# A page table fetched in one transfer and sorted on the chip, in place of 20 small transfers

## The chip, the cores and the metric

The kernel runs on one core of a Trainium2 chip. The metric is the device time of one execution in microseconds (us). Before the change its median over three runs is 2779.84 us (2775.24 to 2781.72).

## The reference: what is computed

One inference step of a two-layer hybrid decoder: a prompt of 16 + 512 tokens and a sample group of 8 sequences with 8 new tokens each, 592 tokens in all, with a model width of 1024. Each layer is a feed-forward block, a mixer and a second feed-forward block. The mixer joins a state-space scan with an attention of eight heads. The sample group's attention also reads 2048 older keys and values for each sequence from a paged cache:

```python
page_table (8, 16) int32          # page_table[b, g]: physical page of sequence b's g-th block of 128 tokens
k_past = cache_k[l][page_table].reshape(8, 2048, 8, 64)
v_past = cache_v[l][page_table].reshape(8, 2048, 8, 64)
```

The page table has 128 entries and is the same for both layers. It is first used in the mixer of layer 0; the feed-forward block that comes ahead of it doesn't need it.

## The kernel before, in words

Activations lie with the model dimension on the 128 partitions and the 592 tokens along the free dimension, as eight tiles `x`. Precision is kept by splitting: each operand becomes a rounded high part and the remainder (`xh`, `xl` for activations, `whi`, `wlo` for weights), and each product is three matmuls, `whi` by `xh`, `whi` by `xl`, `wlo` by `xh` (`mm3`, L585 to L593, two halves of 296 columns).

Weights come in as `raw` tiles of 512 KB (`raw`, L570; three buffers), all issued from SyncE's queue (SP). Each serves two sets of 24 matmuls. For each set ScalarE (ACT) writes `whi` (L581), VectorE (DVE) subtracts and writes `wlo` (L582), and TensorE (PE) multiplies; `whi` and `wlo` have three buffers each. Two PSUM banks hold a pair of halves, and three pairs are in turn.

The norm's factor R, one number a token, is worked out beside the first matmuls: `sq` holds summed squares (L453), matmuls sum them over partitions (L463), ACT copies the sums (L471), PE transposes them (L476), DVE works out a reciprocal root in small steps (`rs`, `rv`, `ry`, `rw`, L494 to L515), PE spreads it (L206), ACT writes `R` (L559). Until R is there no product may leave PSUM (L229 multiplies by R), so PE can fill three pairs and then stands.

`setup` loads the activations; `setup_rest` (L275) prepares all that only the mixer needs and is called from within the first feed-forward block, after the first of its three parts. Each engine works through its own list in order and waits on semaphores. A scheduler that simulates the program fixes the order of each list when the program is built; so an instruction whose inputs seem to be there early can stand in the list long ahead of the place where the source has it.

Two page-table tiles feed the index tiles of the gathers, `ki` (keys, L347) and `vi` (values, L351). Partition p of `ptk` holds, for each of the 8 sequences, the entry of block p // 8; partition p of `ptv` holds, for each sequence and each of four values of a, the entry 4a + p // 32. Both are filled straight from HBM: 16 transfers of 8 partitions by 8 elements (L332) and 4 transfers of 32 partitions by 32 elements (L335), in which neighbours along a partition are not neighbours in HBM. DVE then converts them to float (`kf` L338, `vf` L339), and scales and offsets them (L340 to L351). GpSimd (POOL) issues the gathers (L1462, L1526) in the mixer.

`dtr` (L984) is a small weight tile of the scan, with its split `dtw` on ACT (L989) and DVE (L990); `mt` (L286) holds masks and `dk` (L294) a skip factor.

Of the kernel before, what the change touches and what calls it, by code (L numbers as in the profile page):

```python
# [11 lines left out]
I32 = mybir.dt.int32  # L12
AF = mybir.ActivationFunctionType
ALU = mybir.AluOpType
# [13 lines left out]
def const_arrays():  # L28
    p = np.arange(128)
    f = np.float32  # L30
    a32 = np.arange(32)
    c = {}
    c["ident"] = np.eye(128)
    c["ones"] = np.ones((128, 1))
    c["half"] = p[:, None] // 64 == np.arange(32)[None, :]
    o8 = np.zeros((128, 64))
    q64 = np.arange(64)
    same = q64[:, None] // 8 == q64[None, :] // 8
    o8[:64] = same
    c["one8"] = o8  # L40
    c["srep"] = p[:, None] % 32 == p[None, :] % 32
    a16 = np.arange(16)[None, :]
    c["sel16"] = (p[:, None] % 8 == a16 % 8) & (p[:, None] // 32 % 2 == a16 // 8)
    c["mko"] = ((p[:, None] // 8) % 4 == np.arange(4)[None, :])
    sm = np.zeros((128, 8))
    sm[:64] = q64[:, None] // 8 == np.arange(8)[None, :]
    c["seqm"] = sm
    dsel = np.zeros((128, 8))
    for h in range(8):
        dsel[h, h] = 1.0  # L50
        dsel[32 + h, h] = 1.0
    c["dsel"] = dsel
    c["koff"] = ((p % 8) * 16)[:, None]
    c["voff"] = ((p % 32) * 4)[:, None]
    c["kt16"] = np.broadcast_to(np.arange(16)[None, :], (128, 16))
    return {k: np.ascontiguousarray(v.reshape(128, -1)).astype(f) for k, v in c.items()}

# [47 lines left out]
class Kern:  # L105
# [169 lines left out]
    def setup_rest(self):  # L275
        nc, I = self.nc, self.I
# [4 lines left out]
        n = off["tri"][0]  # L281
# [43 lines left out]
            nc.vector.tensor_copy(o[:, 0], v)  # L325
            nc.vector.tensor_scalar(o[:, 1], v, -1.0, None, ALU.mult)

        ptk = self.cst([128, 8], "ptk", I32)
        ptv = self.cst([128, 32], "ptv", I32)
        pt = I["page_table"]  # L330
        for g in range(16):
            nc.sync.dma_start(ptk[8 * g:8 * g + 8, :], pt[:, g].partition_broadcast(8))  # L332
        ptr = pt.rearrange("b (a x) -> x (b a)", x=4)
        for x in range(4):
            nc.sync.dma_start(ptv[32 * x:32 * x + 32, :], ptr[x].partition_broadcast(32))  # L335
        kf = self.cst([128, 8], "kf")
        vf = self.cst([128, 32], "vf")
        nc.vector.tensor_copy(kf, ptk)  # L338
        nc.vector.tensor_copy(vf, ptv)  # L339
        nc.vector.tensor_scalar(kf, kf, 128.0, self.c_koff, ALU.mult, ALU.add)  # L340
        nc.vector.tensor_scalar(vf, vf, 128.0, self.c_voff, ALU.mult, ALU.add)
        nc.vector.tensor_scalar(kf, kf, 0.5, None, ALU.mult)
# [1230 lines left out]
def build(nc, inputs):  # L1573
    arrays, I, O = {}, {}, {}
    CA, CM = pack(const_arrays()), pack(mask_arrays())
    given = {k: np.ascontiguousarray(inputs[k]) for k in _INS}
    given["c_const"], given["c_mask"] = CA[1], CM[1]
    for name, a in given.items():
        arrays["in_" + name] = a
        I[name] = nc.dram_tensor("in_" + name, a.shape, mybir.dt.from_np(a.dtype), kind="ExternalInput").ap()  # L1580
    for name, shape in _OUTS:
        O[name] = nc.dram_tensor("out_" + name, shape, F32, kind="ExternalOutput").ap()
    with tile.TileContext(nc, schedule_with_timeline_sim=True) as tc:
        with ExitStack() as ctx:
            Kern(tc, ctx, I, O, CA, CM).run()
    return arrays
# [10 lines left out]
```

## Time and profile before

| | |
|---|---|
| median of three runs | 2779.84 us |
| the profiled execution | 2797.72 us |
| its span, first to last instruction | 2795.9 us (1.8 us lie around it) |
| mean granted TensorE clock | 0.973 |
| PE busy | 2656.9 us (95% of the span) |
| DVE busy | 1502.2 us (54%) |
| ACT busy | 994.7 us (36%) |
| POOL busy | 356.9 us (13%) |
| transfers from SP's queue | 213184 packets, 205.71 MB |

A row of the timeline gives start, duration, engine, line and operation, output and inputs; in square brackets stands how long the engine had been idle and what ended that. "PEclk" is the granted TensorE clock as a share of full speed, and "x" in a table of windows counts instructions. The rows that matter stand in the prediction.

### The profile page before, as it was taken

How to read it: one execution, taken by the hardware profiler on the slowest of the kernel's cores; microseconds unless marked ns; L12 is line 12 of the kernel's file. 1: busy time of each engine (PE TensorE's matmuls, PEld its weight loads, DVE VectorE, ACT ScalarE, POOL GpSimd, SP SyncE). 2: the span in 40 equal slices, each digit the busy share in tenths (PEclk: the TensorE clock that was granted, in tenths of full speed). 3: DMA queues.
4: the chain of work that ended last, by engine and by line, in shares of the span. 5: the costliest groups of instructions: out<-in, count | busy, mean ns of one | idle time of the engine just before them, and what ended most of it. 6: DMA issues, size and time to landing. Idle time of an engine off the chain costs nothing.

```text
span 2795.9 us, 51271 instructions
## 1 busy us (share of the span) xinstructions
PE 2656.9 (95%) x21469; PEld 2472.6 (88%) x21469; DVE 1502.2 (54%) x2978; ACT 994.7 (36%) x1795; POOL 356.9 (13%) x336
## 2 busy tenths in 40 slices
PE   6999999999877999999999999999997789999999
PEld 5999999887655899999999999998885568999999
DVE  4444445386768564343554343454776776444444
ACT  2222224255645332222332222233565543322222
POOL 1000000023356010000000000000334541000000
PEclk8999999999979999999999999999998899999999
DMA  3232234347677222222222322244576772222222
GB/s 100 76 93 93 79 106 134 113 145 258 204 233 241 100 69 85 82 76 88 72 84 76 105 77 92 87 145 126 169 248 203 250 236 69 78 89 80 88 77 87
DMA packets 250279, 343.22 MB, mean 123 GB/s; under 512 B 38104, under 2 KB 201888, under 8 KB 250048
## 3 DMA queue, kind: packets, MB, share of 16 engines
q1 hardware_dynamic: 213184, 205.71, 23.8%
q0 software_dynamic: 36864, 134.23, 14.4%
q8 instruction: 168, 2.75, 0.4%
q14 instruction: 63, 0.52, 0.1%
HBM read 320.23 MB, written 19.66 MB: 122 GB/s over the span
## 4 chain that ended last, share of the span: by engine, by line
PE 59%; DVE 3%; ACT 2%; DMA 1%; issue 1%; POOL 0%; another core or an unknown queue 0%; SPq 0%; DVEq 0%; ACTq 0%; POOLq 0%
PE g L590 52%; PE v L905 1%; DMA v<-in_cache_v,vi 1%; DVE kt L1468 1%; PE po L206 1%; PE po L463 0%; PE po L209 0%; PE sc L209 0%; DMA kn<-in_cache_k,ki 0%; PE z L209 0%; POOL v L1526 0%; PE z L206 0%; ACT L1090 0%; ACT dec L1090 0%; DVE x L777 0%
## 5 line engine op out<-in xcount | busy, mean ns | idle before, releaser
L590 PE MATMUL g<-xh,wlo 128*128 128x296 f32 (+1 forms) x3392 | 1014.6, 300 | 17.3 <-DVE wlo L582 17.3
L590 PE MATMUL g<-xl,whi 128*128 128x296 f32 (+1 forms) x3392 | 1015.9, 300 | 2.7 <-DVE xl L441 2.7
L590 PE MATMUL g<-xh,whi 128*128 128x296 f32 (+1 forms) x3392 | 1014.7, 300 | 2.4 <-DVE gs L229 2.0
L581 ACT ACTIVATE whi<-raw 128x512 fp32r<-128x512 f32 (+1 forms) x664 | 413.9, 624 | 1342.5 <-PE g L590 1271.1
L582 DVE TENSOR_TENSOR wlo<-raw,whi 128x512 fp32r<-128x512 f32 (+1 forms) x664 | 450.9, 679 | 614.5 <-ACT whi L581 568.4
L590 PEld LDWEIGHTS g<-xh,wlo 128*128 128x128 f32 x3392 | 640.4, 189 | 20.6 <-DVE wlo L582 17.9
L590 PEld LDWEIGHTS g<-xh,whi 128*128 128x128 f32 x3392 | 640.0, 189 | 10.5 <-issue 6.3
L590 PEld LDWEIGHTS g<-xl,whi 128*128 128x128 f32 x3392 | 640.5, 189 | 7.5 <-DVE xl L441 3.6
L590 PE MATMUL g<-hl,whi 128*128 128x296 f32 (+1 forms) x1408 | 417.9, 297 | 0.0
L590 PE MATMUL g<-hh,wlo 128*128 128x296 f32 (+1 forms) x1408 | 417.7, 298 | 0.0
L590 PE MATMUL g<-hh,whi 128*128 128x296 f32 (+1 forms) x1408 | 416.8, 298 | 0.0
L1462 POOL DMA_INDIRECT kn<-in_cache_k,ki x128 | 134.7, 1052 | 1590.6 <-PE g L590 1104.8
L590 PEld LDWEIGHTS g<-hl,whi 128*128 128x128 f32 x1408 | 265.2, 188 | 0.0
L590 PEld LDWEIGHTS g<-hh,wlo 128*128 128x128 f32 x1408 | 264.3, 188 | 0.0
L590 PEld LDWEIGHTS g<-hh,whi 128*128 128x128 f32 x1408 | 263.9, 188 | 0.0
L1468 DVE STREAM_TRANSPOSE kt<-kn 128x512 f32<-128x512 f32 x256 | 162.9, 681 | 29.0 <-PE pS L1097 7.5
L1526 POOL DMA_INDIRECT v<-in_cache_v,vi x128 | 139.1, 1087 | 252.3 <-DVE kt L1468 121.3
L686 DVE SCALAR_TENSOR_TENSOR x<-g,x 128x296 f32<-128x296 f32 (+1 forms) x192 | 88.2, 464 | 120.5 <-PE g L590 119.9
L229 DVE TENSOR_TENSOR us<-g,R 128x296 f32<-128x296 f32 (+1 forms) x176 | 81.5, 464 | 128.0 <-PE g L590 127.9
L229 DVE TENSOR_TENSOR gs<-g,R 128x296 f32<-128x296 f32 (+1 forms) x176 | 80.7, 464 | 125.9 <-PE g L590 120.0
L673 ACT ACTIVATE hh<-us 128x592 fp32r<-128x592 f32 (+1 forms) x88 | 61.4, 698 | 63.3 <-DVE us L671 63.3
L209 PE MATMUL sc<-kt,qbd 128*32 128x128 f32 x1920 | 79.0, 291 | 3.7 <-issue 3.6
(387 smaller groups left out, 2993.2 us busy)
## 6 DMA issues: line engine op xcount, KB each, us to landing
raw<-in_ffn_w_gu SPq DMA_DIRECT2D x176, 512.0 KB
raw<-in_ffn_w_down SPq DMA_DIRECT2D x80, 512.0 KB
raw<-in_w_in SPq DMA_DIRECT2D x44, 512.0 KB
raw<-in_w_out SPq DMA_DIRECT2D x16, 512.0 KB
spill<-x SPq DMA_DIRECT2D x16, 296.0 KB
x<-spill SPq DMA_DIRECT2D x16, 296.0 KB
raw<-in_ffn_w_down SPq DMA_DIRECT2D x16, 256.0 KB
xt<-in_x_prompt SPq DMA_DIRECT2D x8, 256.0 KB
```

Source lines behind the costliest of these rows:

```text
L206: i = self.nc.tensor.matmul(*a, **k).ins
L209: i = self.nc.tensor.matmul(*a, **k).ins
L229: self.nc.vector.tensor_tensor(tv[0:P, h, :], ps[h][0:P, 0:self.n], rv[0:P, h, :], ALU.mult)
L581: nc.scalar.activation(hi[:, 0:nk], s, AF.Copy)
L582: nc.vector.tensor_tensor(lo[:, 0:nk], s, hi[:, 0:nk].bitcast(F32), ALU.subtract)
L590: nc.tensor.matmul(ps[h][:, 0:self.n], w[:, k, :], self.hv(x)[:, h, :], start=(first and k == 0 and i == 0), stop=(last and k == nk - 1 an ...
L673: nc.scalar.activation(hh[:, a:b], u[:, a:b], AF.Copy)
L686: nc.vector.scalar_tensor_tensor(v, p, 0.5, v, ALU.mult, ALU.add)
L905: nc.tensor.matmul(ps[c], x[:, t0:t0 + 128], w.rearrange("p x c -> p (x c)"), start=(k == 0 and i == 0), stop=(k == 7 and i == 2))
L1462: nc.gpsimd.indirect_dma_start(kn, None, self.kflat, bass.IndirectOffsetOnAxis(ap=self.kidx[l][:, s, i:i + 1], axis=0))
L1468: nc.vector.transpose(kt[:, 2 * u:2 * u + 2].rearrange("p t h i -> p t (h i)"), kns[u][:, :, 256 * quad:256 * quad + 256])
L1526: nc.gpsimd.indirect_dma_start(v.rearrange("p k c -> p (k c)"), None, self.vflat, bass.IndirectOffsetOnAxis(ap=self.vidx[l][:, i, e:e + 1] ...
```

## The change

One transfer brings the whole page table, 128 numbers of 4 bytes, to every one of the 128 partitions (`pti`). DVE converts it to float (`ptf`) and picks what each partition needs: it multiplies by a 0/1 mask (`mg` for keys, `mx` for values, two new constants of 16 and 4 columns) and adds halves together until one entry is left for each output, five instructions for `kf` and three for `vf`. The tiles `ptk` and `ptv` with their 20 transfers go. `pti`, `ptf` and `sel` come from a pool of six rotating buffers that other temporaries use too. What follows (scaling, `ki`, `vi`, the gathers) stays. After the change the lines from L55 to L327 stand 2 further down, and those from L340 on 6 further down.

```diff
+    c["mg"] = p[:, None] // 8 == a16
+    c["mx"] = p[:, None] // 32 == np.arange(4)[None, :]
...
-        ptk = self.cst([128, 8], "ptk", I32)
-        ptv = self.cst([128, 32], "ptv", I32)
-        pt = I["page_table"]
-        for g in range(16):
-            nc.sync.dma_start(ptk[8 * g:8 * g + 8, :], pt[:, g].partition_broadcast(8))
-        ptr = pt.rearrange("b (a x) -> x (b a)", x=4)
-        for x in range(4):
-            nc.sync.dma_start(ptv[32 * x:32 * x + 32, :], ptr[x].partition_broadcast(32))
+        pti = self.tmp("pti", [128, 128], I32)
+        nc.sync.dma_start(pti, I["page_table"].rearrange("b g -> (b g)").partition_broadcast(128))
+        ptf, sel = self.tmp("ptf", [128, 128]), self.tmp("sel", [128, 128])
+        nc.vector.tensor_copy(ptf, pti)
         kf = self.cst([128, 8], "kf")
         vf = self.cst([128, 32], "vf")
-        nc.vector.tensor_copy(kf, ptk)
-        nc.vector.tensor_copy(vf, ptv)
+        for out, m in ((kf, self.c_mg), (vf, self.c_mx)):
+            n, k = out.shape[1], m.shape[1]
+            sv = sel.rearrange("p (a g) -> p a g", g=k)
+            nc.vector.tensor_tensor(sv, ptf.rearrange("p (a g) -> p a g", g=k),
+                                    m.unsqueeze(1).to_broadcast([128, n, k]), ALU.mult)
+            while k > 1:
+                k //= 2
+                d = out.unsqueeze(2) if k == 1 else sv[:, :, 0:k]
+                nc.vector.tensor_tensor(d, sv[:, :, 0:k], sv[:, :, k:2 * k], ALU.add)
```

The engines' lists, built anew, differ in two places. The first is the start. SP's list before, with all 20 page-table transfers (`raw` are weights of the first feed-forward block, `hp` small head parameters):

```order
L278 DMA call<-in_c_const 128x278
L305 DMA hp<-in_dt_bias 128x16
L305 DMA hp<-in_A_log 128x16
L305 DMA hp<-in_sb_bias 128x16
L332 DMA ptk<-in_page_table 8x8x1 x9
L572 DMA raw<-in_ffn_w_gu 128x4x256
L332 DMA ptk<-in_page_table 8x8x1 x7
L572 DMA raw<-in_ffn_w_gu 128x4x256
L335 DMA ptv<-in_page_table 32x32x1 x4
L984 DMA dtr<-in_w_in 128x8x8
L572 DMA raw<-in_ffn_w_gu 128x4x256
```

and now:

```order
L280 DMA call<-in_c_const 128x298
L307 DMA hp<-in_dt_bias 128x16
L307 DMA hp<-in_A_log 128x16
L307 DMA hp<-in_sb_bias 128x16
L990 DMA dtr<-in_w_in 128x8x8
L578 DMA raw<-in_ffn_w_gu 128x4x256
L990 DMA dtr<-in_w_in 128x8x8
L578 DMA raw<-in_ffn_w_gu 128x4x256 x12
```

The page table has left this place, and `dtr` stands ahead of the weights that it stood behind. DVE's list at the same place before, where it works on the first weights and the norm's sums (`sq`) and comes to the small steps of the norm's factor (`rs`):

```order
L453 TENSOR_TENSOR sq<-sq 128x592
L338 CAST kf<-ptk 128x8
...
L339 CAST vf<-ptv 128x32
L341 TENSOR_SCALAR vf<-vf,call 128x32
L582 TENSOR_TENSOR wlo<-raw,whi 128x512
L343 TENSOR_SCALAR vf<-vf 128x32
L582 TENSOR_TENSOR wlo<-raw,whi 128x512
...
L990 TENSOR_TENSOR dtw_1978<-dtr,dtw_1978 128x4x8
L582 TENSOR_TENSOR wlo<-raw,whi 128x512
L494 COPY rs<-po 128x4x2
```

and now:

```order
L996 TENSOR_TENSOR dtw_1966<-dtr,dtw_1966 128x4x8
L447 SCALAR_TENSOR_TENSOR xl<-x_110,par,xh 128x592
L996 TENSOR_TENSOR dtw_1967<-dtr,dtw_1967 128x4x8
L588 TENSOR_TENSOR wlo<-raw,whi 128x512
L447 SCALAR_TENSOR_TENSOR xl<-x_111,par,xh 128x592
L588 TENSOR_TENSOR wlo<-raw,whi 128x512
L459 TENSOR_TENSOR sq<-sq 128x592
L588 TENSOR_TENSOR wlo<-raw,whi 128x512 x3
L500 COPY rs<-po 128x4x2
```

All that reads the page table has gone from between `sq` and `wlo`, and the two `dtw` stand further ahead. The second place is the end of the first part of the feed-forward block, where products of the down projection are added to `x`. On DVE now:

```order
L692 SCALAR_TENSOR_TENSOR x_104<-g_1374,x_104 128x296
L588 TENSOR_TENSOR wlo<-raw,whi 128x512
L334 CAST ptf<-pti 128x128
L340 TENSOR_TENSOR sel<-ptf,call 128x128
L345 TENSOR_TENSOR sel<-sel 128x8x8
L345 TENSOR_TENSOR sel<-sel 128x8x4
L345 TENSOR_TENSOR sel<-sel 128x8x2
L345 TENSOR_TENSOR kf<-sel 128x8
L340 TENSOR_TENSOR sel<-ptf,call 128x128
L346 TENSOR_SCALAR kf<-kf,call 128x8
L588 TENSOR_TENSOR wlo<-raw,whi 128x512
```

Before, the two `wlo` followed each other there. The other nine instructions of the page table follow, among two additions to `x`. SP's list has, at this place, `pti` behind the first weights after `dk`:

```order
L296 DMA dk<-in_D_skip 8x2
L578 DMA raw<-in_ffn_w_down 128x4x256
L332 DMA pti<-in_page_table 128x128
L578 DMA raw<-in_ffn_w_down 128x4x256 x3
```

PE's and ACT's lists change only at the start and by a few places (on ACT the two `dtw`, L989, now stand ahead of the last `sq`, L447); POOL's is the same.

## The prediction

> **What bounds the kernel now.** First the page, for the shares of the engines.
>
> ```profile
> PE 2656.9 (95%) x21469; PEld 2472.6 (88%) x21469; DVE 1502.2 (54%) x2978; ACT 994.7 (36%) x1795; POOL 356.9 (13%) x336
> ```
>
> PE sets the time: it is busy 95% of the span, and elsewhere an edit on another engine is worth nothing unless PE waits for it. So I looked for where PE does not work. The windows of the start (span of the window, then busy time and instructions of PE, PEld, DVE, ACT, POOL, then granted clock, DMA share, GB/s):
>
> ```profile
> 30.00:40.00 10.00, 9.11 (x62) 7.67 (x60) 4.85 (x12) 1.27 (x2) 1.52 (x2) 1.00 0.23 54
> 40.00:50.00 10.00, 0.00 (x0) 0.00 (x0) 0.00 (x0) 0.00 (x0) 0.00 (x0) 0.71 0.18 31
> 50.00:60.00 10.00, 3.38 (x14) 3.36 (x15) 4.10 (x18) 1.48 (x5) 0.00 (x0) 0.50 0.29 67
> 60.00:70.00 10.00, 7.23 (x35) 6.80 (x34) 5.17 (x19) 3.93 (x6) 0.00 (x0) 0.67 0.28 69
> 80.00:90.00 10.00, 10.00 (x76) 10.00 (x75) 4.15 (x8) 2.85 (x5) 0.00 (x0) 1.00 0.25 83
> ```
>
> At full speed PE does 76 matmuls in 10 us. From 40 to 50 no engine works at all, and the DMA engines are 18% busy. The timeline of PE says what ended this, and where PE stood again behind it:
>
> ```profile
> 39.68 0.30 PE L590 MATMUL g<-xl,whi 128*128 128x296 f32 x1
> 56.62 0.61 PE L590 MATMUL g<-xh,wlo 128*128 128x296 f32 x1 [16.64 <-DVE wlo L582]
> ...
> 62.25 0.30 PE L590 MATMUL g<-xh,wlo 128*128 128x296 f32 x1
> 64.35 0.33 PE L206 MATMUL po<-identr,rhi 128*128 128x128 f32 x1 [1.80 <-DVE rhi L514]
> ...
> 67.44 0.62 PE L590 MATMUL g<-xh,whi 128*128 128x296 f32 x1 [0.97 <-DVE gs L229]
> ```
>
> PE's last matmul ended at 39.68 + 0.30 = 39.98; then it waited 16.64 us for `wlo`. `wlo` is a cheap subtraction, so what did DVE do?
>
> ```profile
> 34.65 0.36 DVE L347 SCALAR_TENSOR_TENSOR ki<-kf,call 128x64 int32<-128x64 f32 x2
> 55.51 0.18 DVE L339 CAST vf<-ptv 128x32 f32<-128x32 int32 x1 [20.50 <-DMA ptv<-in_page_table]
> 55.73 0.24 DVE L341 TENSOR_SCALAR vf<-vf,call 128x32 f32<-128x32 f32 x1
> 55.88 0.68 DVE L582 TENSOR_TENSOR wlo<-raw,whi 128x512 fp32r<-128x512 f32 x1
> ```
>
> It stood 20.50 us at `vf`, waiting for the table, with `wlo` next but one in its list. ACT stood as well, for `dtr`, which SP had issued behind `ptv`:
>
> ```profile
> 55.79 0.35 ACT L989 ACTIVATE dtw<-dtr 128x32 fp32r<-128x32 f32 x2 [19.61 <-DMA dtr<-in_w_in]
> ```
>
> SP's rows, and the packets moved from 34 to 44 us:
>
> ```profile
> 32.50 12.40 SPq L335 DMA_DIRECT2D ptv<-in_page_table x4
> 44.94 3.19 SPq L984 DMA_DIRECT2D dtr<-in_w_in x1
> ```
>
> ```profile
> DMA packets 2342, 0.41 MB, mean 41 GB/s; under 512 B 1951, under 2 KB 2342, under 8 KB 2342
> ```
>
> Four transfers of 32 by 32 elements make 4096 elements; issued at 32.50 and awaited until 55.51 they took 23.0 us, 5.6 ns each. In ten of those microseconds 1951 packets under 512 B moved, 5.1 ns each: they go one element at a time. This is a stall by number of pieces, not by bytes.
>
> **The change part by part.** Removed: all 20 transfers, and `vf`'s place ahead of `wlo`. (1) The stall. Without it PE meets `wlo` at 39.98 if `wlo` is there. ACT and DVE say:
>
> ```profile
> 34.72 0.63 ACT L581 ACTIVATE whi<-raw 128x512 fp32r<-128x512 f32 x1 [6.65 <-PE g L590]
> ```
>
> ```profile
> 33.29 0.77 DVE L453 TENSOR_TENSOR sq<-sq 128x592 f32<-128x592 f32 x1
> ```
>
> DVE is free at 34.06, `whi` ends at 35.35, `wlo` (0.68) then at about 36.1, 3.9 us ahead of need. So the 16.64 us go whole.
>
> (2) Behind the stall. From 56.62 to 62.55 PE did the 22 matmuls left of its three pairs and 5 transposes for R, at first at half clock (0.50 in the row of 50 to 60). At full clock, with each taken at 10 us / 76 = 0.132: 27 × 0.132 = 3.6 in place of 5.9, so it ends at 39.98 + 3.6 = 43.6. The restart waits for the small steps of R:
>
> ```profile
> 58.37 0.17 DVE L494 COPY rs<-po 128x8 f32<-128x8 f32 x1
> ...
> 63.11 0.69 DVE L582 TENSOR_TENSOR wlo<-raw,whi 128x512 fp32r<-128x512 f32 x1 [2.07 <-ACT whi L581]
> ```
>
> A `wlo` stands in the middle of them; it waits for a `whi` whose buffer PE frees with its last set. That set's end decides, then, and L206 starts 1.80 us after it as before (62.55 to 64.35), at 45.4. The other branch isn't later: transposes end near 41.2, and the steps ahead of that `wlo` take 58.37 to 61.04 (63.11 − 2.07), 2.7, to 43.9; the wait of 2.07 shrinks, but not the 1.80. Removed by (1) and (2): 64.35 − 45.4 = 18.95, say 19.0 us.
>
> (3) The clock after the restart. Windows of the clock:
>
> ```profile
> 61.00:61.50 0.50, 0.50 (x5) 0.50 (x4) 0.04 (x1) 0.00 (x0) 0.00 (x0) 0.73 0.95 225
> 64.50:64.75 0.25, 0.25 (x3) 0.25 (x4) 0.00 (x0) 0.00 (x0) 0.00 (x0) 0.87 0.00 0
> 71.50:72.00 0.50, 0.50 (x6) 0.50 (x5) 0.17 (x1) 0.00 (x0) 0.00 (x0) 0.99 0.00 0
> ```
>
> Full at about 61.27, half again from 64.72 to 71.5, though PE had stood for only 1.80 us. Of these 6.8 us PE worked all but the pause of 0.97, so full clock would save at most half of 5.8, 2.9 us. The pauses of 1.80 and 0.97 stay, so I take most of the half clock as staying too: gain 0 to 2.9, I take 0.6, a fifth. "TensorE: Matmul & The Clock Gate" of the Trainium skill (Part 1: The HAM clock gate) says that the clock halves after an idle window of about 3.4 us, on a grid that doesn't start with the kernel. By it a pause of 1.8 us shouldn't halve it, and the sum would take the 2.9 whole, 21.7 us in all; the rows differ, since the clock fell 3.45 us after it had risen, with 1.28 us of that worked (61.27 to 62.55).
>
> (4) `dtr` moves ahead. SP would issue it after `hp`, where `ptk`'s row begins:
>
> ```profile
> 15.19 5.48 SPq L332 DMA_DIRECT2D ptk<-in_page_table x9
> 23.38 0.70 ACT L447 ACTIVATE sq<-x 128x592 f32<-128x592 f32 x1 [1.70 <-DVE x L401]
> ```
>
> ACT would reach `dtw` at 23.38 − 1.70 = 21.68 and has these 1.70 us spare there (0.35 for the two `dtw`). `dtr` has 1024 pieces of 32 B: at 5.1 ns, 5.2 us, so it's there at about 20.5; by its own row before (44.94 to 55.79, behind `ptv`) 10.9, so at 26.1. The first costs nothing, the second 26.1 + 0.35 − 23.38 = 3.1 us. I take the first. DVE does two `dtw` (0.29) ahead of the first sets, where it works nine tenths of the time: 0.2 lost.
>
> (5) Added, at the second place. DVE, SP and ACT there before:
>
> ```profile
> 156.88 0.93 SPq L286 DMA_DIRECT2D mt<-in_c_mask x2
> ...
> 159.08 0.38 SPq L572 DMA_DIRECT2D raw<-in_ffn_w_down x1
> ```
>
> ```profile
> 160.77 0.44 DVE L287 CAST mall<-mt 128x544 bf16<-128x544 f32 x1 [1.71 <-DMA mt<-in_c_mask]
> ...
> 162.18 0.67 DVE L582 TENSOR_TENSOR wlo<-raw,whi 128x512 fp32r<-128x512 f32 x1
> 164.84 0.69 DVE L582 TENSOR_TENSOR wlo<-raw,whi 128x512 fp32r<-128x512 f32 x1 [2.00 <-ACT whi L581]
> ```
>
> ```profile
> 164.17 0.64 ACT L581 ACTIVATE whi<-raw 128x512 fp32r<-128x512 f32 x1 [2.58 <-PE g L590]
> ```
>
> `pti` is issued behind the 512 KB of 159.08, at 159.5; `mt` in like place took 3.9 us from issue to use, so 163.4; DVE comes to `ptf` at 162.85 and waits 0.6. Then eight instructions stand ahead of the next `wlo`. From 0.77 for 592 elements and 0.17 for 5, one costs 0.17 + 1.02 ns an element: 0.30 (128, three times), 0.23, 0.20, 0.18, 0.17, and a scaling 0.24 (row of 55.73), 1.9 us, with 0.03 between them 2.2. So `wlo` starts at 165.6, 0.8 late. ACT wrote its `whi` when PE freed the buffer at 164.1; with three buffers two sets (2 × 24 × 0.132 = 6.3 us) lie between, so PE needs `wlo` at 170.7 and it may start until 170.0. Cover 4.4 us: cost 0; without that cover it would be 2.8 (0.6 + 2.2). Queued behind are the nine other instructions (about 2.0 us by the same rule) and two additions to `x`, whose PSUM pair PE wants back two pairs (12 us) later. The 20 columns more of constants are 10 KB. POOL's first gather waits for `ki`, now 130 us longer; behind it is only
>
> ```profile
> 202.56 0.94 POOL L1462 DMA_INDIRECT kn<-in_cache_k,ki  x1 [165.66 <-PE g L590]
> ```
>
> which waits for PE until then anyway. Cost 0.
>
> Sum: 19.0 + 0.6 − 0.2 = 19.4 us. Bounds: 19.0 − 0.2 − 3.1 = 15.7 to 19.0 + 2.9 − 0.2 = 21.7. The profiled execution would come from 2797.72 to 2778.3. It is 17.9 us longer than the median; taking the same stall in runs without a profile, 2779.84 − 19.4 = **2760.4 us**, own range with the runs' scatter of some 3 us 2755 to 2767.
>
> **Rivals.** (A) *The stall is partly the profiler's.* It records each packet, and 4096 tiny ones in a row may be slowed; the 17.9 us between profiled run and median leave room. Against: 213184 packets of this queue were recorded, and elsewhere PE runs through. If half the gain is so, 9.7 us are left: 2770. 13%.
> (B) *Another wait takes its place at the start*: `dtr` late on ACT, a weight tile late, or R's chain by more than I found. By twice the bound of `dtr`, 6.2 us: gain 13.2, 2767. For it: ACT has only 1.70 us spare at `dtw`; against it, each row above leaves some us of lead. 11%.
> (C) *The stall was covering a wait that comes anyway*, so that nothing is gained: PE can't go beyond three pairs without R. Against: in ACT's list the copy of R's sums stands right behind `dtw`, whose wait for `dtr` ended only at 55.79, so R's chain was held by the same transfers. 2777 to 2782, 4%.
> (D) *Slower*: `pti`, 16384 elements, goes element by element as `ptv` did. At 5.1 ns that is 84 us from 159.5 on, and with 2.2 + 0.7 the next `wlo` is there at 246, where PE needs it at 170.7: 2779.84 − 19.4 + 75 = 2835. It decides from a landing 28 us after the issue (159.5 + 27.7 + 2.9 = 170.7 + 19.4). Against: each row is 512 B in a piece, and `mt`, 69632 elements in long rows, was there in 3.9 us. 3%.
> (E) *The clock stays full behind the start*, since the 16.64 us that cooled it are gone. For it: PE works from 20 to 43.6 nearly without a pause; against it, the fall at 64.72 after 1.80 us. Gain 19.0 + 2.9 − 0.2 = 21.7: 2758.1, 12%.
> (F) The change does not do what it says: the list still has a page-table wait ahead of `wlo` at the start. The lists above exclude it.
>
> **How the numbers follow.** Forecast 57%, A 13, B 11, C 4, D 3, E 12. About 0.2% (5.6 us) is what a measurement here can tell from no change. Faster by more: 57 + 12 + 11 + 12 of A's 13 (a gain under 5.6 is left to its rest) = 92%; same: C and that rest, 5%; slower 3%. The range takes in E and B and reaches to the middle of A: 2753 to 2770.
>
> **What would show it.** Right: DVE's wait of 20.50 us at the start is gone; PE's L206 starts near 45.5, the next L590 near 48.5; PE stands nowhere over 1 us between 140 and 155; `ptf` waits under 2 us. Behind 70 us the whole trace is shifted by one constant, 16 to 22 us. Step 2 is wrong if PE's pause ahead of L206 grows, step 4 if ACT waits for `dtr`, step 5 if PE waits for a `wlo` near 150. The prediction is wrong if PE's first three pairs still end in a pause of several us, or if profiled and timed runs gain differently by more than 4 us.

## The result: 22.0 us faster in a first comparison, 13.7 us in a second

| | us |
|---|---|
| the kernel before, beside it | 2779.51 (2775.24 to 2781.72, 4 runs) |
| the changed kernel | 2757.47 (2754.89 to 2758.84, 4 runs) |
| ratio | 0.9925, 95% interval 0.9906 to 0.9944 |
| profiled execution of the changed kernel | 2756.55, span 2754.8, clock 0.977 |

The forecast was 2760.4. The changed kernel was measured a second time later (its own section below): ratio 0.9954, interval 0.9937 to 0.9971. So the two medians differ by 22.0 and 13.7 us, and the intervals allow 16 to 26 and 8 to 17. What the change itself does can be read much more sharply from the traces, because away from the start and the second place both kernels run the same lists. One run of a kernel below (the rows at the start) took 8464.58 us, three times the others; it is left out of that kernel's ratio, and what held it isn't known.

### The profile page after: what moved, and what is told of

Read it like the earlier page. It is cut to its first block, busy times and chain, and to the rows that moved or that the text cites. A ratio compares the mean times of both kernels' runs of the same rounds, so it can differ in the third digit from the quotient of the medians.

```text
span 2754.8 us, 51256 instructions
## 1 busy us (share of the span) xinstructions
PE 2640.9 (96%) x21469; PEld 2466.1 (90%) x21469; DVE 1506.4 (55%) x2985; ACT 994.0 (36%) x1795; POOL 361.5 (13%) x336
## 4 chain that ended last, share of the span: by engine, by line
PE 59%; DVE 3%; DMA 2%; ACT 2%; issue 1%; POOL 0%; SPq 0%; DVEq 0%; POOLq 0%; ACTq 0%
PE g L596 53%; DMA v<-in_cache_v,vi 1%; PE v L911 1%; DVE kt L1474 1%; DMA kn<-in_cache_k,ki 1%; PE po L208 1%; PE po L469 1%; PE po L211 0%; DVE x L783 0%; PE sc L211 0%; PE z L211 0%; DVE st L1279 0%; PE z L208 0%; PE zt L1331 0%; PE zo L211 0%
## 5 line engine op out<-in xcount | busy, mean ns | idle before, releaser
L596 PE MATMUL g<-mh,whi 128*128 128x296 f32 (+1 forms) x256 | 78.3, 312 | 3.5 <-DVE ot L231 2.0
```

What stands on the lines that cost most here:

```text
L596: nc.tensor.matmul(ps[h][:, 0:self.n], w[:, k, :], self.hv(x)[:, h, :], start=(first and k == 0 and i == 0), stop=(last and k == nk - 1 an ...
```

## The profile after

First the windows of the start (columns as in the prediction: PE, PEld, DVE, ACT, POOL, clock, DMA share, GB/s):

```profile
30.00:40.00 10.00, 9.40 (x68) 8.44 (x67) 5.00 (x9) 2.53 (x5) 0.00 (x0) 1.00 0.40 109
40.00:50.00 10.00, 7.12 (x44) 6.74 (x43) 7.02 (x27) 4.05 (x7) 0.00 (x0) 0.83 0.17 54
50.00:60.00 10.00, 10.00 (x74) 10.00 (x74) 5.16 (x8) 3.17 (x5) 0.00 (x0) 1.00 0.16 51
```

The window from 40 to 50, in which nothing worked before, now has 44 matmuls. PE's timeline there:

```profile
42.65 0.30 PE L596 MATMUL g<-xh,wlo 128*128 128x296 f32 x1
44.75 0.33 PE L208 MATMUL po<-identr,rhi 128*128 128x128 f32 x1 [1.80 <-DVE rhi L520]
...
47.16 0.62 PE L596 MATMUL g<-xh,whi 128*128 128x296 f32 x1 [1.08 <-DVE gs L231]
```

The three pairs end at 42.95 without a stall, the wait for R is 1.80 us as before, and the first product behind R starts at 47.16 where it started at 67.44. What SP, ACT and DVE do (`dtr` now comes ahead, the third pair's `wlo` stands at 35.12):

```profile
15.08 0.38 SPq L990 DMA_DIRECT2D dtr<-in_w_in  x1
```

```profile
21.29 0.34 ACT L995 ACTIVATE dtw<-dtr 128x32 fp32r<-128x32 f32 x2
22.99 0.70 ACT L453 ACTIVATE sq<-x 128x592 f32<-128x592 f32 x1 [1.37 <-DVE x L407]
```

```profile
32.66 0.77 DVE L459 TENSOR_TENSOR sq<-sq 128x592 f32<-128x592 f32 x1
35.12 1.29 DVE L588 TENSOR_TENSOR wlo<-raw,whi 128x512 fp32r<-128x512 f32 x2 [1.69 <-ACT whi L587]
```

ACT does not wait for `dtr`; DVE waits for `whi`, and PE for neither. At the second place:

```profile
139.12 0.33 SPq L332 DMA_DIRECT2D pti<-in_page_table  x1
```

```profile
142.80 0.23 DVE L334 CAST ptf<-pti 128x128 f32<-128x128 int32 x1 [0.78 <-DMA pti<-in_page_table]
...
144.63 0.69 DVE L588 TENSOR_TENSOR wlo<-raw,whi 128x512 fp32r<-128x512 f32 x1
147.35 0.68 DVE L588 TENSOR_TENSOR wlo<-raw,whi 128x512 fp32r<-128x512 f32 x1
150.60 0.69 DVE L588 TENSOR_TENSOR wlo<-raw,whi 128x512 fp32r<-128x512 f32 x1 [2.56 <-ACT whi L587]
```

The rows are there 3.7 us after their issue, `ptf` waits 0.78, and by 150.60 DVE waits for `whi` again, so it has caught up; PE stands nowhere there.

**How far this shift reaches.** Two instructions of DVE serve as marks: `cot`, a copy in layer 0's mixer, and `hl`, a step of the feed-forward block behind it, where the work is steady again. Before, then after:

```profile
600.99 0.53 DVE L977 COPY cot<-cop 27x384 f32<-27x384 f32 x1
...
1075.03 0.78 DVE L674 TENSOR_TENSOR hl<-us,hh 128x592 fp32r<-128x592 f32 x1 [0.17 <-ACT hh L673]
```

```profile
580.16 0.54 DVE L983 COPY cot<-cop 27x384 f32<-27x384 f32 x1
...
1037.37 0.78 DVE L680 TENSOR_TENSOR hl<-us,hh 128x592 fp32r<-128x592 f32 x1 [0.16 <-ACT hh L679]
```

At `cot` the changed kernel is 20.83 us ahead, at `hl` 37.66. The first is the change: where DVE first reads gathered keys (389.1 us before, 368.3 after) the shift is the same 20.8. The other 16.8 us come up inside the mixer (474.04 us from `cot` to `hl` against 457.21), which the change doesn't touch, and they are not in the timed runs. Most of the experiments bear on one of these two numbers.

## Experiments

All times are medians of 5 to 12 runs, but for the kernel before profiled again, which ran once; the ratio is to the kernel before, run beside each on the same chip. The first four and the last three ran on one chip (here: chip A), the four between on another (chip B).

### Only the values

```diff
-        for x in range(4):
-            nc.sync.dma_start(ptv[32 * x:32 * x + 32, :], ptr[x].partition_broadcast(32))
+        pti = self.tmp("pti", [128, 128], I32)
+        nc.sync.dma_start(pti, I["page_table"].rearrange("b g -> (b g)").partition_broadcast(128))
...
-        nc.vector.tensor_copy(vf, ptv)
+        for out, m in ((vf, self.c_mx),):
```

The 16 transfers into `ptk` and the conversion into `kf` stay.

> Only the values' half of the change: the 16 transfers for the keys stay (1024 one-element pieces), the 4 for the values (4096 pieces) go, and the values are made from the 128 rows at the second place. My theory (the stall is ptv's 4096 pieces, with dtr queued behind them): kf found its table without a wait before, so it will again. SP issues dtr at about 32.5 us instead of 44.9; its 1024 pieces take 5.2 to 10.9 us, so DVE's dtw, which stands ahead of the third pair's wlo in its list, goes at 37.7 to 43.4, and PE, which needs that wlo at 40.0, waits 0 to 4 us. Gain 17 to 22 us: 2758 to 2763. Rival (the 16 small transfers cost as much as the 4, by number of transfers): the stall at the start stays at over half, gain under 10 us, over 2770.

2757.04 us against 2779.16, ratio 0.9927 (0.9907 to 0.9946): the whole gain. In its timelines of ACT and PE:

```profile
35.26 0.35 ACT L1000 ACTIVATE dtw<-dtr 128x32 fp32r<-128x32 f32 x2 [7.47 <-DMA dtr<-in_w_in]
```

```profile
44.40 0.33 PE L208 MATMUL po<-identr,rhi 128*128 128x128 f32 x1 [1.80 <-DVE rhi L525]
```

ACT waits 7.47 us for `dtr`, issued at 31.64, but is done at 35.6, ahead of PE's need; L208 is even 0.35 earlier than in the changed kernel. The 16 transfers for the keys show no cost. All of the gain comes from the four that are gone.

### Only the keys

```diff
-        for g in range(16):
-            nc.sync.dma_start(ptk[8 * g:8 * g + 8, :], pt[:, g].partition_broadcast(8))
+        pti = self.tmp("pti", [128, 128], I32)
+        nc.sync.dma_start(pti, I["page_table"].rearrange("b g -> (b g)").partition_broadcast(128))
...
-        nc.vector.tensor_copy(kf, ptk)
+        for out, m in ((kf, self.c_mg),):
```

The 4 transfers into `ptv` and the conversion into `vf` stay.

> Only the keys' half of the change: the 16 transfers go, the 4 for the values stay and are issued right behind hp, at about 15.2 us, ahead of dtr and two weight tiles. My theory (23.0 us for 4096 pieces, and all that is behind them in the queue waits): ptv is there at about 38.2 and dtr right behind it, at 38.5 to 43.4; ACT, whose dtw stands ahead of its squares, is held from 21.7 until then, and DVE at vf from about 30. PE loses 10 to 17 us at an earlier place than before; gain 4 to 10 us: 2769 to 2776. Rival (the issue time of the transfers is the cost, 12.4 us for the four and 8 us for the 16): dtr is there by 33, PE loses under 6 us, gain over 15 us: below 2765.

2792.43 us, ratio 1.0045 (1.0027 to 1.0062): 13 us slower than before, which no theory had. Its timelines of DVE, ACT and PE:

```profile
36.53 0.18 DVE L341 CAST vf<-ptv 128x32 f32<-128x32 int32 x1 [6.88 <-DMA ptv<-in_page_table]
```

```profile
37.98 0.35 ACT L1000 ACTIVATE dtw<-dtr 128x32 fp32r<-128x32 f32 x2 [16.63 <-DMA dtr<-in_w_in]
```

```profile
40.17 0.61 PE L601 MATMUL g<-xh,whi 128*128 128x296 f32 x1 [12.27 <-ACT whi L592]
...
58.11 0.33 PE L208 MATMUL po<-identr,rhi 128*128 128x128 f32 x1 [2.00 <-DVE rhi L525]
```

The start went as expected. `ptv`, issued at 14.90, took 21.6 us; `dtr` was held behind it and came 1.4 us later; PE lost 12.27 us in an earlier place; L208 is 6.2 us earlier than before. At `cot` (593.82) this kernel is 7.2 us ahead of the kernel before, within the 4 to 10 that were expected. The 20 us that turn this into a loss arise behind it; the last section of experiments finds them.

### The table read late

```diff
-        nc.vector.tensor_copy(kf, ptk)
-        nc.vector.tensor_copy(vf, ptv)
+        for out, src in ((kf, ptk), (vf, ptv)):
+            self.tc.add_manual_dep(nc.vector.tensor_copy(out, src).ins, late.name, order, reason="late")
```

`late` is the copy that reads `dk`, at 160 us.

> The kernel before with all its 20 transfers at the start, but the two instructions that read them (kf, vf) forced to the second place, behind 160 us. So DVE no longer stands at vf. My theory (the whole queue is held: dtr comes behind ptv, and ACT's dtw, the copy of R's sums behind it, and DVE's dtw all wait for dtr): ACT and DVE stand until 55.8 as before, PE has two wlo more and finishes most of its three pairs by 43, but R's chain starts at 56 and L206 comes at 60 to 62 instead of 64.35. Gain 1 to 5 us: 2775 to 2779. Rival (vf's wait in DVE's list is the whole cause): the stall goes, gain 16 to 20 us, 2760 to 2764.

2778.14 us, ratio 1.0003 (0.9988 to 1.0017): no gain. ACT and PE:

```profile
55.81 0.35 ACT L990 ACTIVATE dtw<-dtr 128x32 fp32r<-128x32 f32 x2 [19.97 <-DMA dtr<-in_w_in]
```

```profile
56.69 1.11 PE L477 MATMUL po<-call,sums 128*128 128x128 f32 x4 [16.77 <-ACT sums L472]
...
57.67 0.59 PE L591 MATMUL g<-xl,whi 128*128 128x296 f32 x1
...
62.43 0.30 PE L591 MATMUL g<-xh,wlo 128*128 128x296 f32 x1
64.53 0.33 PE L206 MATMUL po<-identr,rhi 128*128 128x128 f32 x1 [1.79 <-DVE rhi L515]
```

DVE no longer stands at `vf`, and yet PE stands 16.77 us, now for `sums`, the next in ACT's list behind `dtw`, which waits for `dtr`, which waits behind the 4096 pieces. L206 comes at 64.53 (64.35 before); my 60 to 62 was too hopeful. In PE's list the transposes of `sums` stand ahead of the last 20 matmuls of the three pairs, so PE still had those to do behind the wait, at half clock for most of them (57.67 to 62.73), though their `whi` and `wlo` had been there since 36.6. Two waits end at nearly the same time here, at 55.5 and 55.8 us; to take one away gives nothing.

### The small transfers at the second place

```diff
-        ptk = self.cst([128, 8], "ptk", I32)
-        ptv = self.cst([128, 32], "ptv", I32)
+        ptk = self.tmp("ptk", [128, 8], I32)
+        ptv = self.tmp("ptv", [128, 32], I32)
```

The two tiles now come from the rotating buffers, as `pti` does in the changed kernel, and the lists have their transfers at the second place.

> The kernel before with its 20 transfers of single elements, but at the second place, where the change has its block; the start is then as in the changed kernel. My theory (pieces cost, at 5.6 ns each, wherever the engines wait for them): behind mt (136.1) the 16 issues take 9.8 us, ptv is issued from about 147 and there at about 170; DVE stands at vf for over 20 us with wlo behind it, PE stops near 152 to 154 and goes on at 171, with 1 to 3 us of half clock behind it: 17 to 23 us of the gain are given back: 2774 to 2781. Rival (only the place counted: at the second place there is lead enough for the small transfers): PE waits under 5 us, 2757 to 2763.

2777.69 us, ratio 0.9998 (0.9984 to 1.0013): the gain is gone. The timelines of DVE and PE, and the windows:

```profile
177.18 0.18 DVE L339 CAST vf<-ptv 128x32 f32<-128x32 int32 x1 [21.22 <-DMA ptv<-in_page_table]
```

```profile
178.91 0.61 PE L590 MATMUL g<-hh,wlo 128*128 128x296 f32 x1 [14.24 <-DVE wlo L582]
```

```profile
160.00:170.00 10.00, 4.66 (x35) 4.42 (x33) 0.00 (x0) 1.26 (x2) 0.00 (x0) 0.90 0.22 53
170.00:180.00 10.00, 1.09 (x4) 1.10 (x5) 2.72 (x9) 0.00 (x0) 0.00 (x0) 0.50 0.07 1
```

The start is as clean as in the changed kernel, and the same stall stands 120 us later: issued at 153.04, used at 177.18, 24.1 us for 4096 pieces. PE stands 14.24 us for `wlo`, about 10 us later than I had expected. At `cot` (598.80) the trace is 18.6 us later than the changed kernel's. So the gain is that of the pieces, not of the place.

### Twice the pieces

```diff
+        pt2 = self.cst([128, 32], "pt2", I32)
-        for x in range(4):
-            nc.sync.dma_start(ptv[32 * x:32 * x + 32, :], ptr[x].partition_broadcast(32))
+        for t in (pt2, ptv):
+            for x in range(4):
+                nc.sync.dma_start(t[32 * x:32 * x + 32, :], ptr[x].partition_broadcast(32))
```

> The kernel before with the values' 4 transfers issued twice, into two tiles, of which only the second is read: 4096 one-element pieces more at the start. My theory (5.6 ns a piece, one after the other, in runs without a profile as well): everything behind the stall is 21 to 24 us later, 2800 to 2804. Rival (the stall is partly the profiler's, which records each packet): the timed runs grow by half of it or less, under 2792, while the profiled start still shows some 23 us more. Second rival (the transfers overlap, and only their issue of 12.4 us counts): 10 to 14 us more, 2790 to 2794.

2819.09 us against 2801.28, ratio 1.0064 (1.0046 to 1.0082): 17.8 us more in the timed runs, under the 21 to 24 expected. DVE and PE of its profile:

```profile
75.66 0.18 DVE L341 CAST vf<-ptv 128x32 f32<-128x32 int32 x1 [38.99 <-DMA ptv<-in_page_table]
```

```profile
81.49 0.48 PE L206 MATMUL po<-identr,rhi 128*128 128x128 f32 x1 [38.20 <-DVE rhi L516]
```

8192 pieces from 32.29 to 75.66 are 5.3 ns each, and `vf` is 20.15 us later than before, L206 17.1. The difference of 3 us is work that PE did in the stall, since in this list two `wlo` stand ahead of `vf`. Timed (17.8, by the interval 13 to 23) and profiled (17.1 at L206, 17.7 at `cot`) agree, so the recording of packets isn't what makes the pieces slow: half of the profiled cost or less lies outside that interval, and the first rival of the prediction falls. That the transfers overlap and only their issue counts (10 to 14) is ruled out by the 20.15 us at `vf`; the timed runs alone would just leave room for it.

### The rows in sixteen transfers

```diff
-        nc.sync.dma_start(pti, I["page_table"].rearrange("b g -> (b g)").partition_broadcast(128))
+        for g in range(16):
+            nc.sync.dma_start(pti[8 * g:8 * g + 8, :],
+                              I["page_table"].rearrange("b g -> (b g)").partition_broadcast(8))
```

> The changed kernel with its one transfer cut into 16, of 8 rows of 512 B each (the same bytes and the same 128 pieces). My theory (pieces count, not transfers): the issues take 0.33 to 0.61 us each, 5 to 10 us in all, so the rows are there 5 to 10 us later, which the lead at the second place (4.4 us) covers in part: 2757 to 2763. Rival (the number of transfers was the cost, 20 against 1): 15 us or more are given back, over 2772.

2782.22 us against 2801.28 on that chip, ratio 0.9927 (0.9908 to 0.9946): the whole gain again. SP and DVE:

```profile
140.37 6.30 SPq L333 DMA_DIRECT2D pti<-in_page_table  x16
```

```profile
149.18 0.22 DVE L336 CAST ptf<-pti 128x128 f32<-128x128 int32 x1
```

Sixteen issues take 6.30 us, 0.39 each, DVE finds the rows there, and PE doesn't stand. The lead that the expectation counted on was not drawn upon: in DVE's list, built anew, `ptf` stands behind two more `wlo` than in the changed kernel. The absolute 2757 to 2763 that was expected was worked out from chip A; the ratio is what holds.

### The kernel before, profiled again

No edit.

> The kernel before, unchanged, for a second profile. The profile of before that is shown was of an execution of 2797.72 us, some 18 us over the timed runs, and against the changed kernel's it is some 17 us longer in layer 0's mixer too, where the change touches nothing. My theory (this is a difference between executions): a second profiled execution of the same kernel has the same stall at the start, 16 to 17 us, but lacks most of the 17 us in the mixer: 2775 to 2785. Rival (the change shortens the mixer as well): it has them again, and lies near 2797.

2794.15 us, on chip B, where the timed runs of the same kernel lie from 2793.31 to 2809.62 (median 2801.28). Its two marks:

```profile
600.99 0.53 DVE L977 COPY cot<-cop 27x384 f32<-27x384 f32 x1
...
1070.77 0.78 DVE L674 TENSOR_TENSOR hl<-us,hh 128x592 fp32r<-128x592 f32 x1 [0.16 <-ACT hh L673]
```

`cot` stands at 600.99 in both profiles; the mixer takes 469.78. My expectation of 2775 to 2785 missed, and so did its reason: this is no chance of one execution, since all 17 timed runs lie there. It goes with the chip, though chip B was used in one session only: on chip A the same kernel takes 2775 to 2780 (medians of three comparisons, the first put there by its time). The profile that the prediction was made from (mixer 474.04) looks like one of chip B; which chip it ran on isn't recorded.

### The rows at the start, and a surprise

```diff
-        pti = self.tmp("pti", [128, 128], I32)
-        ptf, sel = self.tmp("ptf", [128, 128]), self.tmp("sel", [128, 128])
+        self.car = [self.cst([128, 128], f"car{i}") for i in range(2)]
+        self.tot = [self.cst([128, 128], f"tot{i}") for i in range(2)]
+        pti, ptf, sel = self.car[0].bitcast(I32), self.car[1], self.tot[0]
```

The block borrows tiles of the scan, which are filled with 1.0 behind it; so it need not wait for the rotating buffers.

> The changed kernel with its block put at the start, where the 20 transfers were: the row transfer behind hp at about 14.7 us, ahead of dtr, and the steps on DVE between its work for the first pairs (the buffers are those of four tiles that are filled later). My theory (pieces cost, not the place): the 128 rows are there within 4 to 5 us, as mt was, no engine waits for them, and DVE's 4 us more of work mostly fit ahead of the wlo that PE needs at 40.0; R's steps may begin up to 2 us later. 2757 to 2760, within 0.1% of the changed kernel. Rival (the gain is that the table left the start): 3 us or more of the gain are lost, over 2761.

2801.25 us against 2801.28, ratio 0.9998 (0.9984 to 1.0011): no gain at all, although the start is the one expected:

```profile
45.15 0.33 PE L208 MATMUL po<-identr,rhi 128*128 128x128 f32 x1 [2.21 <-DVE rhi L518]
```

At `cot` (581.73) the kernel is 1.57 us behind the changed kernel and 19.3 ahead of the one before. At `hl` it is 8.7 us behind the kernel before on that chip (1070.77):

```profile
1079.42 0.77 DVE L678 TENSOR_TENSOR hl<-us,hh 128x592 fp32r<-128x592 f32 x1 [0.16 <-ACT hh L677]
```

497.69 us in the mixer. The rival ("the gain is that the table left the start") seems to win, but for a wrong reason: nothing was lost at the start. Laid side by side, the lists showed what this kernel and the one with only the keys changed have in common: behind the first thousand rows of PE's list, 659 and 1020 rows differ from the changed kernel's, in the mixers. In the other kernels, the one before among them, none does. The program's scheduler, which simulates the program, had laid out the mixers in another order.

### One cast

Two kernels separate the place of the rows from the order of the mixers. The first has the row transfer at the start and its steps where the changed kernel has them (against the kernel above, one line, apart from the names `late` and `order` that it uses); its lists of PE and ACT are those of the changed kernel:

```diff
-        nc.vector.tensor_copy(ptf, pti)
+        self.tc.add_manual_dep(nc.vector.tensor_copy(ptf, pti).ins, late.name, order, reason="late")
```

> The changed kernel with its row transfer at the start, behind hp, and its steps on DVE still at the second place (a forced order). Behind the start the lists of all engines are those of the changed kernel. Two kernels so far, with the row block or the keys at the start, lost some 20 us in the mixers, where the lists of PE, DVE, ACT and POOL had come out in another order (659 and 1020 rows of PE's list differ behind its first thousand); the seven with the same lists there didn't. My theory (the place of the rows is free; the order in the mixers cost the 20 us): as the changed kernel, ratio 0.991 to 0.995, L208 at 44.5 to 45.5. Rival (rows at the start cost by themselves, wherever that shows): ratio 0.998 or more.

The second adds one cast at the start whose output nothing reads:

```diff
+        nc.vector.tensor_copy(self.tot[1], pti)
```

> The kernel before this one in the list with one instruction more: a cast of the 128 rows at the start, 0.23 us on DVE, whose output nothing reads. With it the program's planner puts the mixers in the other order, that of the kernel with only the keys changed. My theory (the order in the mixers costs 19 to 21 us): L208 within 0.5 us of the run without the cast, the trace shifted by under 1 us until 600 us, and then some 20 us lost between 600 and 1000 us: ratio 0.998 to 1.002. Rival (the loss of those two kernels came from elsewhere, such as the early gathers or the start): as the run without the cast, 0.991 to 0.995.

Beside them the changed kernel once more:

> The changed kernel, unchanged, beside the two. Ratio 0.991 to 0.995 again. Where the kernel before runs near 2779 us, it is near 2757; where before runs near 2801 us, near 2780, with the difference between the two in the paged gathers of the mixers and the start alike.

| kernel | us | ratio (95%) |
|---|---|---|
| before | 2775.23 | |
| rows at the start, steps late | 2759.91 | 0.9948 (0.9934 to 0.9962) |
| the same and one cast | 2777.20 | 1.0008 (0.9997 to 1.0020) |
| changed kernel again | 2761.56 | 0.9954 (0.9937 to 0.9971) |

One instruction of 0.23 us costs 17.3 us. At the start it costs 0.64 (L208 at 45.23 and 45.87), a little over the 0.5 expected. The marks and a window of the kernel without the cast, then with it:

```profile
581.84 0.54 DVE L982 COPY cot<-cop 27x384 f32<-27x384 f32 x1
...
1039.63 0.78 DVE L679 TENSOR_TENSOR hl<-us,hh 128x592 fp32r<-128x592 f32 x1 [0.16 <-ACT hh L678]
```

```profile
900.00:950.00 50.00, 48.92 (x345) 44.26 (x344) 30.91 (x67) 18.98 (x31) 4.94 (x3) 0.97 0.17 53
```

```profile
582.46 0.53 DVE L983 COPY cot<-cop 27x384 f32<-27x384 f32 x1
...
1061.27 0.77 DVE L680 TENSOR_TENSOR hl<-us,hh 128x592 fp32r<-128x592 f32 x1 [0.17 <-ACT hh L679]
```

```profile
900.00:950.00 50.00, 39.44 (x363) 27.76 (x362) 19.28 (x51) 12.10 (x23) 12.45 (x12) 0.76 0.42 140
```

At `cot` the two are 0.62 us apart, at `hl` 21.64. Without the cast the gathers' tail is over by 900 us (DMA share 0.17) and PE is busy 48.92 of the 50 us at a clock of 0.97; with it the tail goes on (0.42), PE has gaps and the clock is 0.76. In POOL's list (equal rows left out) the gathers `kn` and `v` stand otherwise among the steps `be` of the scan; first without, then with the cast:

```
kn x8, be, v x2, be x2, v x2, be x3, v x4, kn x8, ...
kn x8, v x2, be x2, v x2, be x2, v, be, v x2, be, v, kn x5, be, kn x3, ...
```

The lists of PE, ACT and DVE change with it, so the runs show that the order costs this, not which exchange in it does. With the mixers' lengths from `cot` to `hl` in all 13 profiles the pieces fall into place:

| layer 0's mixer, us | order of the changed kernel and of the one before | the other orders |
|---|---|---|
| chip A | 457.2 (changed), 457.0 (changed, again), 457.8 (rows at the start, steps late), 453.8 (only the values), 454.0 (read late), 453.7 (pieces late) | 479.3 (only the keys), 478.8 (one cast) |
| chip B | 469.8 (before), 475.8 (sixteen transfers), 478.0 (twice the pieces) | 497.7 (rows at the start) |

The order costs 21 to 26 us on chip A and 20 to 28 on B; the chip costs some 12 to 24, with one profile behind each number. In layer 1's mixer the lists of the three kernels on the right differ as well, but nothing is lost there: from `hl` to the last instruction all 13 profiles take 1714 to 1726 us. The changed kernel's first two runs, timed and profiled, are put under chip A by the times of the kernel before beside them; the first profile of before (474.04) stands outside the table. The expected ratio of the changed kernel (0.991 to 0.995) was just missed at 0.9954, with an interval that reaches into it. Why the group of 454 and that of 457 differ by some 3.5 us isn't settled.

No kernel here beats the changed one: the one with only the values changed is 0.35 us ahead of it at the start, which no timing can tell.

## Why the prediction was right

**Step 1, the stall goes whole: right.** 16.64 us are gone, and the reason was tested from four sides: without `ptv` all is gained, with it elsewhere it is lost there, doubled it costs nearly as much again, and without DVE's wait but with the queue unchanged nothing is gained. The last shows that the words "so R's chain was held by the same transfers" carry more than I gave them: I had them only in the third rival's counter-argument, though getting `dtr` out from behind `ptv` is as necessary as taking away the wait at `vf`.

**Step 2, behind the stall: right.** The three pairs end at 42.95 (43.6 forecast), the pause ahead of L208 is 1.80 us as forecast, L208 starts at 44.75 (45.4): 19.6 us for steps 1, 2 and 4 together in place of 18.8. Two executions of one kernel differ by nearly as much. In the second profile of the changed kernel, without an edit, L208 comes 0.5 us later, 19.1 us ahead of before:

```profile
45.26 0.33 PE L208 MATMUL po<-identr,rhi 128*128 128x128 f32 x1 [1.79 <-DVE rhi L520]
```

Most of this is there ahead of all that the change moves: the same `xl` of DVE starts at 18.70 and at 19.16 (before, at 19.09).

**Step 3, the clock: a term that hangs on luck.** I took 0.6 of at most 2.9 us. From L208 (19.60) to `cot` (20.83) 1.2 were gained. The windows of the clock after:

```profile
43.22:46.63 3.41, 1.33 (x10) 1.19 (x10) 1.32 (x6) 0.88 (x3) 0.00 (x0) 1.00 0.05 17
46.50:47.00 0.50, 0.00 (x0) 0.00 (x0) 0.36 (x1) 0.48 (x3) 0.00 (x0) 0.63 0.00 0
46.63:50.04 3.41, 2.88 (x12) 2.88 (x12) 3.10 (x7) 2.83 (x5) 0.00 (x0) 0.50 0.00 0
50.00:50.50 0.50, 0.50 (x5) 0.50 (x5) 0.00 (x0) 0.50 (x1) 0.00 (x0) 0.96 0.00 0
```

From 0.63 and 0.96 the clock fell at about 46.63 and rose at about 50.04: one stretch of 3.4 us at half clock in place of 6.8 before. The pauses were the same, as I had said, but not where they fell in the clock's windows. The kernel with sixteen transfers, with the same list of PE and pauses of 1.80 and 1.03 us, shows the other case:

```profile
45.50:46.00 0.50, 0.50 (x6) 0.50 (x5) 0.00 (x0) 0.00 (x0) 0.00 (x0) 0.96 0.00 0
45.96:49.37 3.41, 2.38 (x11) 2.19 (x11) 2.57 (x7) 3.27 (x5) 0.00 (x0) 0.50 0.02 5
52.50:53.00 0.50, 0.50 (x5) 0.50 (x4) 0.00 (x0) 0.00 (x0) 0.00 (x0) 0.72 0.00 0
```

There the clock fell at about 45.96 and rose at about 52.78, 6.8 us as before the change, and between L208 (19.54) and `cot` (19.60) only 0.1 was gained. In the first 3.41 us behind the fall PE had worked 2.38 us, and the clock stayed at half; in the changed kernel it had worked 2.88, and the clock rose. The second profile of the changed kernel has 3.4 us and 1.1 gained, the rows at the start with late steps 6.8 and 0.0. So the term is 0 to 1.2 us, by where an execution meets the clock's windows, and my 0.6 lies in the middle of that by luck, not by its reason.

"TensorE: Matmul & The Clock Gate" of the Trainium skill (Part 1: The HAM clock gate) has windows of about 3.4 us on a free-running grid; the length agrees with 3.4 and twice 3.4 here. Its rule that the clock falls after an idle window does not: in the 3.41 us ahead of the fall PE worked 1.33. In the profile before it had worked 1.65 of the 3.45, not the 1.28 that I gave: the 0.37 from 64.35 on belong to it too. The fifth rival, a clock that stays full, came true in neither profile of the changed kernel.

**Step 4, `dtr` ahead: right.** There without a wait at 21.29, 6.2 us after its issue at the latest; the bound of 3.1 wasn't needed.

**Step 5, the second place: right.** `ptf` waits 0.78 (0.6 forecast) and `wlo` is caught up by 150.60; PE stands nowhere. Cost 0.

**The sum** was 19.4; the trace shows 20.8 at the end of everything that the change touches (20.2 in the second profile of the changed kernel): 0.8 of the miss from step 2 with step 4, 0.6 from step 3. The timed medians, 2757.47 and 2761.56 against a forecast of 2760.4, are too coarse to judge a term under a us.

**The test that it failed.** I had written that the prediction is wrong if profiled and timed runs gain differently by more than 4 us. They do: 41.2 (2797.72 to 2756.55) against 22.0. The step behind that test, that the profiled execution's extra 17.9 us have nothing to do with the stall, holds: they lie in the mixer, and on chip B, where the timed runs too are that long, the ratio is the same (0.9927 with sixteen transfers). But the two profiled executions could not be compared by their totals, and I had no reason to think they could. That the trace would be shifted by one constant behind 70 us was right only up to 600 us.

**Rivals.** Profiler (first): refuted by the doubled pieces. Another wait at the start (second): none. A wait that comes anyway (third): true of the kernel with the late read, not of the change. Row by element (fourth): `pti` was there in 3.7 us. What no rival had is the largest risk that the runs showed: a new instruction at the start can reorder the mixers 500 us later and cost all of the gain. The changed kernel escaped it; three of its neighbours didn't. That its lists differ from those before in two places only was known ahead of the result; that 20 us hung on it was not.

## What to carry to other kernels

Count a transfer's pieces, not its bytes or its instructions: a table whose neighbours in the tile are not neighbours in memory went one element at a time here, at over 5 ns each, and the tile behind it in the same queue waited too, so look at what is queued behind before you move the reader. Where a scheduler lays out the program, compare the whole lists after an edit, not those near the edit: edits that did at the start what was expected of them lost 20 us in a stage they never touched. And compare traces by marks in the program, piece by piece, before you compare two totals.

## What was not expected of the hardware

- One-element pieces cost 5.3 to 5.9 ns each in every place they were tried (21.6, 23.0 and 24.1 us for 4096, 43.4 for 8192), while 128 rows of 512 B in one transfer took 3.7 us in all.
- The clock fell after a stretch in which PE had worked 1.33 of 3.41 us; no idle stretch of that length was needed. It stayed at half when PE had worked 2.38 of the next 3.41 us and rose when it had worked 2.88.
- Two chips run the same kernel 22 to 26 us apart (medians 2775 to 2780 and 2801). 12 to 24 us of it lie in layer 0's mixer (the table above); from `hl` to the last instruction, some 1720 us with layer 1's mixer among them, the profiles of both chips lie within 12 us.
